# Seven half-size block products for eight in the gate/up stages of a float32 decoder trunk

## The chip, the core and the metric

The kernel runs on one core of one Trainium2 chip. Its time is the device time of one execution in microseconds (us); the number given for a kernel is the median of several runs. Five engines work side by side, each through its own list of instructions in a fixed order: PE (TensorE, matrix products), DVE (VectorE) and ACT (ScalarE) (element by element), POOL (GpSimd, element by element, SBUF only) and SP, which here issues the loads. They wait for one another by semaphores only.

## The reference

Two layers work on 512 tokens of width 1024 in float32. Each layer has four sub-layers: a SwiGLU feed-forward network with weight 1/2, a token mixer, a second such network, and a gated embedding. All of them are normalised before and after, and added to the residual. The change touches the feed-forward networks alone, of which there are four:

```python
def swiglu(x, w_gate, w_up, w_down):
    return (jax.nn.silu(x @ w_gate) * (x @ w_up)) @ w_down

h = rmsnorm(x, g_ffn1_pre[i])
x = x + 0.5 * rmsnorm(swiglu(h, w1_gate[i], w1_up[i], w1_down[i]), g_ffn1_post[i])
```

`w_gate` and `w_up` are 1024 x 2816, `w_down` is 2816 x 1024.

## The kernel before

**Layout.** Activations lie with features on the 128 partitions and tokens in the columns: 1024 features are eight slabs of 128 x 512 (`xs`), the 2816 hidden features 22 slabs (`hid`). A weight tile of 128 x 128 is the stationary operand of a matrix product, 512 tokens (or 256, where a stage is done in token halves) are the moving one.

**Exact halves.** Every float32 operand is cut in two: `h`, its rounding to a shorter type that PE takes at full rate, and `l`, what is left. A product of two operands is three matmuls into one PSUM bank: high by high, low by high, high by low (`product`, lines 255 to 257). ACT makes the high part (`halves`, line 239, `wh`), DVE or POOL the low part by a subtraction (line 240, `wl`); the letter `on` says which engine. For an activation `split` does the same (lines 174 and 175, `h` and `l`). Every weight is loaded once (`load_raw`, 256 KB a load, line 233, four buffers) and has its halves made in eight buffers of 128 x 512 for `wh` and eight for `wl`.

**A feed-forward network** (`ffn`) is a gate/up stage and a down stage. The gate/up stage goes over 22 M-tiles of 128 hidden features. Each has a gate product and an up product over all eight slabs of `xs`: 2 x 8 x 3 = 48 matmuls of 512 columns, with four loads of weights and their halves. `activate` then multiplies both PSUM banks by `rb`, the tokens' 1/rms as a row on every partition (lines 556 and 558, DVE), applies silu (line 557, ACT), multiplies gate by up (line 559, DVE), and cuts the result in halves. The down stage has eight M-tiles of 22 x 3 = 66 matmuls; the last is done in two token halves, so that the post-norm of the first half runs beside the products of the second (`finish`).

**Entry.** `Entry` brings the residual `x` up to date slab by slab, first for tokens 0 to 255, then for 256 to 511, and makes its halves (`xh` on ACT, line 415; `xl` on DVE, line 418). The first three products of the next stage follow slab by slab in token halves (`products`); a fourth needs no `rb`. The sums of squares give `rb` some time later.

**What sets the order.** The loads, the matmuls and the element-wise work are written in the order of the program; a list scheduler of the framework then fixes each engine's order when the kernel is built, within the limits of the buffers. Only a few stretches are pinned by hand (`manual_schedule`, `issue_after`).

Of the kernel before, what the change touches and what calls it, by code (L numbers as in the profile page):

```python
# [34 lines left out]
# M-tiles done in token halves where a sub-layer starts and where it ends  # L35
# [6 lines left out]
# engines of the first weights' differences  # L42
# [10 lines left out]
# engines (a, v, g) of the mixer's copies and differences  # L53
# [24 lines left out]
HID_TAGS = {"s": "m" * 8 + "a" * 10 + "s" * 4, "m": "a" * 10 + "s" * 12}  # L78
# [7 lines left out]
# output projection: order of the K-slabs, and how many of them each M-tile takes early  # L86
# [10 lines left out]
# columns of the small-parameter array, per layer  # L97
# [10 lines left out]
# columns of the constants array  # L108
# [26 lines left out]
def hybrid_trunk(ctx: ExitStack, tc: tile.TileContext, a: dict, out: bass.AP):  # L135
# [83 lines left out]
    # ---- weights: DMA, then exact halves  # L219
    def load_w(src, slabs, cols, on="vv"):  # L220
# [3 lines left out]
        return [w for k0 in range(0, slabs, per)  # L224
                for w in halves(load_raw(src[:, k0:min(k0 + per, slabs)], cols), on[k0 // per % len(on)])]
# [5 lines left out]
    def load_raw(src, cols):  # L231
        raw = wtile("raw", src.shape[1], cols, F32)
        nc.sync.dma_start(out=raw, in_=src)
        return raw

    def halves(raw, on="v"):
        _, n, cols = raw.shape
        h, lo = wtile("wh", n, cols, F32R), wtile("wl", n, cols, F32R)
        A.copy(out=h, in_=raw)  # L239
        (G if on == "g" else V).tensor_tensor(out=lo, in0=raw, in1=f(h), op=ALU.subtract)  # L240
        return [(h[:, k], lo[:, k]) for k in range(n)]
# [6 lines left out]
    def product(o, w, xs, first=True, cols=slice(0, S), tick=lambda: None, last=True):  # L248
        """o[:, cols] = sum over slabs; a bank's later columns are not `first`."""
# [10 lines left out]
    def start():  # L260
        """The first normalized input and the first weights, as they arrive."""
# [25 lines left out]
        first = [(w[t, 0] + w[t, 1], bank()) for t in range(3)]  # L287
# [7 lines left out]
        rt, rb = rstd(sq.parts(), D)  # L295
        return SimpleNamespace(xs=xs, rt=rt, rb=rb, first=first)

    # ---- norms
    def rsqrt_cols(o, v4, inv_d, between):
# [10 lines left out]
        mul, add, sub = ALU.mult, ALU.add, ALU.subtract  # L310
        for op, kw in (
            (V.tensor_scalar, dict(out=v, in0=v4, scalar1=inv_d * lam, scalar2=EPS * lam, op0=mul, op1=add)),
# [11 lines left out]
            between()  # L324

    class Rstd:
# [3 lines left out]
        def __init__(self, dim, cols=slice(0, S), tag="v"):  # L330
            self.dim, self.blocks, self.st, self.tag = dim, blocks(cols), None, tag

# [10 lines left out]
        def col(self, between=lambda: None):  # L343
            n = len(self.blocks)
            self.rt = tp.tile([P, n], F32, tag=f"rt{n}", name="rt", bufs=4)
            rsqrt_cols(self.rt, self.st, 1.0 / self.dim, between)
# [9 lines left out]
    def rstd(sqs, dim, tag="v"):  # L356
        r = Rstd(dim, tag=tag)
# [9 lines left out]
    class Squares:  # L367
        """Sums of squares over M-tiles, for the tokens `cols`."""
# [29 lines left out]
    class Entry:  # L398
        """A sub-layer's input: x * gain as exact halves, and rstd. `update(k, cols)` first brings
        x[k] up to date; `row_b()` makes what it needs for the later half of the tokens."""  # L400
# [25 lines left out]
        def products(self, tiles, more=lambda: None):  # L426
            """tiles: (weights, bank) of the first M-tiles, in token halves; `more()`: further
            products that need no rstd."""
# [11 lines left out]
            r = Rstd(D)  # L440
# [8 lines left out]
        def later(self):  # L449
            """Conversions of later weights queue behind those of the input."""  # L450
# [5 lines left out]
    def finish(ys, sq, last, compute, evac, gcol, nxt, at, xtag="s"):  # L456
        """The last M-tiles in token halves, each half's post-norm during the other's products;
        then the residual, and the next sub-layer's input."""
        rb = slot(name="rbs")
        direct = {m: slot(name="sq") for m in list(last)[-DIRECT:]}  # L460
# [13 lines left out]
        ra, rb_ = Rstd(D, ca), Rstd(D, cb)  # L474
# [28 lines left out]
        def row_b():  # L503
            rb_.row(rb[:, cb], None)
# [40 lines left out]
    # ---- sub-layers  # L545
    def ffn(l, idx, state, nxt, xtag="s", early=None):
        xs = state.xs
        hid, banks = [], {}
        order = [(m, j) for m in range(NF) for j in range(2)]

        def weights(m, j, on="vv"):
            return load_w(a[f"w{idx + 1}_gu"][l, m, j], NK, P, on)

        def activate(m):
            g1, u1 = slot(name="g1"), slot(name="u1")
            V.tensor_tensor(out=g1, in0=banks[m, 0], in1=rb, op=ALU.mult)  # L556
            A.activation(out=g1, in_=g1, func=AF.Silu)
            V.tensor_tensor(out=u1, in0=banks[m, 1], in1=rb, op=ALU.mult)  # L558
            V.tensor_tensor(out=u1, in0=g1, in1=u1, op=ALU.mult)  # L559
            hid.append(split(u1, HID_TAGS[xtag][m]))  # L560

        def one(m, j):
            w, b = weights(m, j), bank()
# [3 lines left out]
        def more():  # L567
            for t in order[FIRST:FIRST + MORE]:
                with state.later():
                    w = weights(*t)  # L570
                banks[t] = bank()
                product(banks[t], w, xs)

        done = len(order[:FIRST])
        if l == 0 and idx == 0:
            first = state.first
            round_constants()
        else:
            first = [(weights(*t, on), bank()) for t, on in zip(order[:FIRST], (ON_FFN1, ON_FFN2)[idx].split())]
            state.products(first, more)  # L580
            done += MORE
# [3 lines left out]
        for i, (m, j) in enumerate(order):  # L585
            if (m, j) == (2, 0) and early is not None:
                early()
            if i >= done:
                one(m, j)
            if j:  # L590
                activate(m)
# [6 lines left out]

        for m in range(NK - LAST_DOWN):
            o = bank()  # L600
            product(o, down(m), hid)
# [17 lines left out]
        return finish(ys, sq, last, compute, evac, lambda k: half[:, l, idx, k:k + 1], nxt, AT_DOWN)  # L619

    def trig():
        """cos and signed sin of the rotary angles, [32 * 4 rows, tokens]"""
# [48 lines left out]
    # stick-breaking attention, scores transposed: keys on partitions  # L671
    def sb_head(h, q, k, v, mix):
# [5 lines left out]
        # banks of key blocks; columns are queries j*P .. S  # L678
# [132 lines left out]
    def mixer(l, state, nxt):  # L811
# [51 lines left out]
        # stick-breaking values and the rotary key, tokens on partitions  # L863
# [304 lines left out]
```

## Time and profile before

| | |
|---|---|
| runs of the kernel before | 2185.63, 2184.93, 2184.9 us; median 2184.93 |
| profiled execution, first to last instruction | 2182.0 us (its own device time is not listed; the span is 2.9 us under the median) |
| PE / PEld | 2113.9 us (97%) / 1797.3 us (82%), 10672 matmuls |
| DVE, ACT, POOL | 1264.4 us (58%), 888.5 us (41%), 381.4 us (17%) |
| mean granted PE clock | 0.986 |
| read from memory | 183.65 MB, 85 GB/s over the span |

The page of a profile gives busy times by engine, a chart of 40 slices, and the chain of work that ended last. The groups list instructions of one line, engine and shape with their number, busy time, mean duration in ns and the idle time ahead of them. The timeline gives starts and durations; like rows that follow one another are merged, with their count. The windows give busy time by engine in a stretch. A matmul's recorded duration covers its way through the array, so that matmuls overlap in the records: what one costs is the distance from its start to the next one's.

### The profile page before, as it was taken

To read this page: it belongs to the slowest core of one execution; us is meant where nothing else is said; L and a number is where in the kernel's file an instruction comes from. 1 tells how busy PE (TensorE), PEld (TensorE's weight loads), DVE (VectorE), ACT (ScalarE), POOL (GpSimd) and SP (SyncE) were. 2 spreads that over 40 slices of the span, in tenths; PEclk is the share of its full clock that TensorE was granted. 3 is DMA by queue.
4 is the path that set the end of the run, shared out by engine and by line. 5 is a ranking of instruction groups with operands and counts; after the bars stand their busy time and mean duration, and the time that the engine had idled before them with its cause. 6 is when DMAs were issued, how large, how long until landed. Compare 5 with 4: busy or idle time off the path is not lost.

```text
span 2182.0 us, 29065 instructions
## 1 busy us (share of the span) xinstructions
PE 2113.9 (97%) x10672; PEld 1797.3 (82%) x10672; DVE 1264.4 (58%) x2291; ACT 888.5 (41%) x1696; POOL 381.4 (17%) x354
## 2 busy tenths in 40 slices
PE   8999999999999999999999999999999999999996
PEld 7888888887888888888888888888878888888886
DVE  7644434878877444336774443357788764443376
ACT  5333323545554333224543332235555543332243
POOL 1000002126331000003320000031263400000043
PEclk9999999999999999999899999999999999999998
DMA  5222332311113223332222233322111132223322
GB/s 181 97 97 97 93 98 71 95 55 50 54 42 104 97 97 97 92 100 80 78 93 97 98 97 92 97 67 97 56 53 47 44 107 97 96 95 96 96 73 68
DMA packets 108286, 187.63 MB, mean 86 GB/s; under 512 B 12144, under 2 KB 22640, under 8 KB 108144
## 3 DMA queue, kind: packets, MB, share of 16 engines
q1 hardware_dynamic: 107424, 185.12, 26.9%
q8 instruction: 83, 1.36, 0.2%
q10 hardware_dynamic: 720, 0.67, 0.1%
q14 instruction: 59, 0.48, 0.1%
HBM read 183.65 MB, written 2.10 MB: 85 GB/s over the span
## 4 chain that ended last, share of the span: by engine, by line
PE 86%; DVE 11%; ACT 1%; issue 1%; DMA 0%; POOL 0%; DVEq 0%; ACTq 0%; POOLq 0%
PE ps L256 22%; PE ps L257 22%; PE ps L255 22%; DVE x L516 2%; PE in L255 2%; PE in L256 2%; PE in L257 2%; DVE xl L418 2%; DVE wl L240 1%; PE wo L255 1%; PE wo L256 1%; PE wo L257 1%; PE st L340 1%; DVE y L513 1%; PE z L718 1%
## 5 line engine op out<-in xcount | busy, mean ns | idle before, releaser
L239 ACT CAST wh<-raw 128x512 fp32r<-128x512 f32 (+3 forms) x718 | 428.3, 602 | 818.6 <-PE ps L256 710.8
L240 DVE TENSOR_TENSOR wl<-raw,wh 128x512 fp32r<-128x512 f32 (+3 forms) x677 | 468.5, 697 | 479.8 <-ACT wh L239 476.8
L256 PE MATMUL ps<-xl,wh 128*128 128x512 f32 (+1 forms) x1688 | 627.5, 374 | 11.6 <-DVE xl L418 11.6
L255 PE MATMUL ps<-xh,wh 128*128 128x512 f32 (+1 forms) x1688 | 618.0, 374 | 9.6 <-ACT wh L239 6.6
L257 PE MATMUL ps<-xh,wl 128*128 128x512 f32 (+1 forms) x1688 | 625.5, 372 | 0.0
L392 POOL TENSOR_TENSOR sq<-sq 128x256 f32<-128x256 f32 (+1 forms) x165 | 170.7, 1036 | 1573.3 <-ACT sq L382 1570.5
L256 PEld LDWEIGHTS ps<-xl,wh 128*128 128x128 f32 x1688 | 321.6, 191 | 68.7 <-DVE xl L418 14.8
L255 PEld LDWEIGHTS ps<-xh,wh 128*128 128x128 f32 x1688 | 318.4, 191 | 65.1 <-ACT wh L239 6.6
L257 PEld LDWEIGHTS ps<-xh,wl 128*128 128x128 f32 x1688 | 321.7, 191 | 54.2 <-DVE wl L240 0.3
L255 PE MATMUL ps<-h,wh 128*128 128x512 f32 (+1 forms) x824 | 302.6, 367 | 0.0
L256 PE MATMUL ps<-l,wh 128*128 128x512 f32 (+1 forms) x824 | 302.2, 367 | 0.4 <-DVE l L175 0.4
L257 PE MATMUL ps<-h,wl 128*128 128x512 f32 (+1 forms) x824 | 302.0, 367 | 0.0
L256 PEld LDWEIGHTS ps<-l,wh 128*128 128x128 f32 x824 | 155.4, 189 | 26.1 <-DVE l L175 1.1
L257 PEld LDWEIGHTS ps<-h,wl 128*128 128x128 f32 x824 | 155.4, 189 | 25.4 <-DVE wl L240 0.5
L255 PEld LDWEIGHTS ps<-h,wh 128*128 128x128 f32 x824 | 155.4, 189 | 25.1
L558 DVE TENSOR_TENSOR u<-ps,rb 128x512 f32<-128x512 f32 x88 | 60.7, 690 | 115.4 <-PE ps L257 115.4
L556 DVE TENSOR_TENSOR g<-ps,rb 128x512 f32<-128x512 f32 x88 | 60.8, 690 | 113.9 <-PE ps L257 111.9
L256 PE MATMUL in<-xl,wh 128*128 128x512 f32 (+1 forms) x288 | 103.1, 363 | 4.6 <-DVE xl L418 4.6
L257 PE MATMUL in<-xh,wl 128*128 128x512 f32 (+1 forms) x288 | 102.5, 361 | 0.0
L255 PE MATMUL in<-xh,wh 128*128 128x512 f32 (+1 forms) x288 | 99.8, 366 | 1.5 <-ACT xh L415 1.5
L174 ACT CAST h<-u 128x512 fp32r<-128x512 f32 x88 | 54.5, 620 | 112.6 <-DVE u L559 112.5
L175 DVE TENSOR_TENSOR l<-u,h 128x512 fp32r<-128x512 f32 x88 | 60.5, 691 | 50.9 <-ACT h L174 50.9
(284 smaller groups left out, 2589.4 us busy)
## 6 DMA issues: line engine op xcount, KB each, us to landing
raw<-in_w_gu SPq DMA_DIRECT2D x352, 256.0 KB, 2.5
raw<-in_w_down SPq DMA_DIRECT2D x160, 256.0 KB, 2.6
raw<-in_win_f SPq DMA_DIRECT2D x60, 256.0 KB, 2.7
raw<-in_ple_gate SPq DMA_DIRECT2D x32, 256.0 KB, 2.6
raw<-in_wo_a SPq DMA_DIRECT2D x18, 256.0 KB, 2.8
raw<-in_w_down SPq DMA_DIRECT2D x32, 128.0 KB, 2.1
raw<-in_wo_b SPq DMA_DIRECT2D x12, 256.0 KB, 2.7
raw<-in_win_t SPq DMA_DIRECT2D x16, 144.0 KB, 2.2
```

The costliest lines, as they stand in the source:

```text
L174: A.copy(out=h, in_=src)
L175: V.tensor_tensor(out=lo, in0=src, in1=f(h), op=ALU.subtract)
L239: A.copy(out=h, in_=raw)
L240: (G if on == "g" else V).tensor_tensor(out=lo, in0=raw, in1=f(h), op=ALU.subtract)
L255: T.matmul(oc, wh, xh[:, cols], start=first and k == 0, stop=False, **kw)
L256: T.matmul(oc, wh, xl[:, cols], start=False, stop=False, **kw)
L257: product.last = T.matmul(oc, wl, xh[:, cols], start=False, stop=last and k == n - 1, **kw)
L392: G.tensor_tensor(out=self.acc[:, c], in0=self.acc[:, c], in1=self.last[:, c], op=ALU.add)
L418: iv = V.scalar_tensor_tensor(out=lo, in0=x[k][:, c], scalar=g, in1=f(h), op0=ALU.mult, op1=ALU.subtract)
L516: V.scalar_tensor_tensor(out=x[k][:, c], in0=ys[k][:, c], scalar=gcol(k), in1=x[k][:, c], op0=ALU.mult, op1=ALU.add)
L556: V.tensor_tensor(out=g1, in0=banks[m, 0], in1=rb, op=ALU.mult)
L558: V.tensor_tensor(out=u1, in0=banks[m, 1], in1=rb, op=ALU.mult)
```

## The change

Take one M-tile. Let the input be cut in four blocks, a11, a12, a21, a22: the first index is the token half (256 tokens each), the second the half of the 1024 features (four slabs each). Let the weights be cut in b11 (gate, first four slabs), b21 (gate, last four), b12 and b22 (the same for up). Gate is a11 b11 + a12 b21 and a21 b11 + a22 b21 for the two token halves, up the same with b12 and b22: eight block products. The changed kernel uses the seven-product form of Strassen and Winograd for M-tiles 2 to 21 (class `Unit`, 20 of 22 in each of four stages):

- input forms, once a stage (`input_forms`): s1 = a21 + a22, s2 = a11 - s1, s3 = a11 - a21, s4 = a12 + s2, each with its exact halves (`fh`, `fl`);
- weight forms, for every unit: t1 = b12 - b11, t2 = t1 - b22, t3 = b22 - b12, t4 = b21 + t2. Seven operands (b11, b21, b22, t1 to t4) then need their exact halves, where four did;
- seven products p1 to p7 of 4 slabs x 3 matmuls of 256 columns. p1, p6, p5 and p3 run on in one PSUM bank (`ux`), p7 and p4 in another (`uy`), p2 in a third (`uz`); after each of p1, p6, p5 and p3 ACT copies the running sum out, after p2, p5 and p4 DVE adds.

`ON_FORM` puts the low parts of b11, b21, b22 and t3, and the subtraction that makes t3, on POOL, the rest on DVE. In the first two units of a stage all of it is on DVE (`ON_FORM_NEW`). `up` is no longer multiplied by `rb`: the missing factor by token goes through down into the post-norm, whose epsilon is divided by the same factor (`eps`, a few operations on 128 x 4 values).

The hidden values of the units are kept whole, in one slot each, and cut in halves only ahead of down (`late`). Down's first two M-tiles run side by side, hidden slab by hidden slab (`TOGETHER`). M-tiles 0 and 1 stay plain.

```diff
+    class Unit:
...
+        def __init__(self, src, forms, z, tag, form_on, t3_on):
+            self.forms, self.tag, self.form_on, self.t3_on = forms, tag, form_on, t3_on
+            self.raw = {n: load_raw(src[j][:, k0:k0 + 4], P, tag)
+                        for n, j, k0, tag in (("b11", 0, 0, None), ("b21", 0, 4, None),
+                                              ("b12", 1, 0, "a"), ("b22", 1, 4, "a"))}
...
+        def form(self, n):
+
+            r = self.raw
+            if n == "t2":
+                r["t1"], r["t2"] = (aslot(name="tw").rearrange("p (a b) -> p a b", a=4) for _ in range(2))
+                tt("v", r["t1"], r["b12"], r["b11"], ALU.subtract)
+                tt("v", r["t2"], r["t1"], r["b22"], ALU.subtract)
+            elif n == "t3":
+                r["t3"] = r["b12"]
+                tt(self.t3_on, r["t3"], r["b22"], r["b12"], ALU.subtract)
+            elif n == "t4":
+                r["t4"] = r["b21"]
+                tt("v", r["t4"], r["b21"], r["t2"], ALU.add)
+            return halves(r[n], self.form_on[n])
...
+            for k, ((wh, wl), (xh, xl)) in enumerate(zip(w, self.forms[xn])):
+                T.matmul(o, wh, xh, start=first and k == 0, stop=False, **kw)
+                T.matmul(o, wh, xl, start=False, stop=False, **kw)
+                T.matmul(o, wl, xh, start=False, stop=k == 3, **kw)
...
+        def p4(self, rb):
+            o, g = self.product("y", "t4", "a22", False), self.g
+            V.tensor_tensor(out=g[:, 256:512], in0=o, in1=g[:, 256:512], op=ALU.add)
+            V.tensor_tensor(out=g, in0=g, in1=rb, op=ALU.mult)
+            A.activation(out=g, in_=g, func=AF.Silu)
+            V.tensor_tensor(out=g, in0=g, in1=self.u, op=ALU.mult)
+            return g
...
-            V.tensor_tensor(out=u1, in0=banks[m, 1], in1=rb, op=ALU.mult)
-            V.tensor_tensor(out=u1, in0=g1, in1=u1, op=ALU.mult)
-            hid.append(split(u1, HID_TAGS[xtag][m]))
+            V.tensor_tensor(out=g1, in0=banks[m, 1], in1=g1, op=ALU.mult)
+            hidden(g1)
...
+            if u:
+                u.p1()
+                u.p2()
+            if prev:
+                prev.p3()
+            if u:
+                u.p6()
+            if prev:
+                hidden(prev.p4(rb))
+            if u:
+                u.p7()
+                u.p5()
+            prev = u
+        hid += [split(h, t) for h, t in zip(late, HID_HALVES[EARLY_HID:])]
...
+        together = [bank() for _ in range(TOGETHER)]
```

How the engines' orders move is seen at three places. The first is DVE in the middle of a gate/up stage (first network of layer 0). Before, one M-tile has eight instructions there: four low parts of weights, the two products with `rb`, gate by up, and the low part of the result.

```order
L240 TENSOR_TENSOR wl<-raw,wh 128x512 x2
L558 TENSOR_TENSOR u_1222<-ps,rb 128x512
L240 TENSOR_TENSOR wl<-raw,wh 128x512
L559 TENSOR_TENSOR u_1222<-g_1221,u_1222 128x512
L175 TENSOR_TENSOR l<-u_1222,h 128x512
L240 TENSOR_TENSOR wl<-raw,wh 128x512
L556 TENSOR_TENSOR g_1305<-ps,rb 128x512
```

Now a unit has eleven there. `tw` is t1 or t2, `raw<-raw,tw` is t4, `wl` a low part; `uy` and `uz` are PSUM banks; `g1` and `u1` are the gate and up values of a unit, and the numbers tell buffers apart.

```order
L182 TENSOR_TENSOR tw_2454<-raw_2395,raw_2391 128x512
L263 TENSOR_TENSOR wl_2318<-tw_2314,wh_2317 128x512
L182 TENSOR_TENSOR raw_2252<-raw_2252,tw_2314 128x512
L263 TENSOR_TENSOR wl_2336<-raw_2111,wh_2335 128x512
L182 TENSOR_TENSOR tw_2455<-tw_2454,raw_2397 128x512
L688 TENSOR_TENSOR g1_1976<-uy_2078,g1_1976 128x256
L689 TENSOR_TENSOR g1_1976<-g1_1976,rb_273 128x512
L263 TENSOR_TENSOR wl_2374<-tw_2313,wh_2373 128x512
L691 TENSOR_TENSOR g1_1976<-g1_1976,u1_1977 128x512
L182 TENSOR_TENSOR tw_2595<-raw_2536,raw_2532 128x512
L681 TENSOR_TENSOR u1_2118<-uy_2219,u1_2118 128x256
L670 TENSOR_TENSOR g1_2258<-uz_2282,g1_2258 128x256
```

Eight of the eleven read two operands from SBUF, all 128x512 (t1, t2, t4, three low parts, the product with `rb`, gate by up; the tenth row shown is already the next unit's t1); the other three read a PSUM bank and one operand from SBUF, 128x256.

The second place is POOL in the same stretch. Before, it has nothing there. Now each unit has five instructions on it: the low parts of b11, b21, b22 and t3, and the subtraction that makes t3 (`raw<-raw,raw`).

```order
L263 TENSOR_TENSOR wl_2402<-raw_2391,wh_2401 128x512
L263 TENSOR_TENSOR wl_2420<-raw_2393,wh_2419 128x512
L182 TENSOR_TENSOR raw_2536<-raw_2538,raw_2536 128x512
L263 TENSOR_TENSOR wl_2438<-raw_2256,wh_2437 128x512
L263 TENSOR_TENSOR wl_2498<-raw_2395,wh_2497 128x512
```

All five are 128x512 and read both operands from SBUF.

The third place is DVE at the entry to the second network of layer 0, between the last slab of the input (`xl_7370`, slab 7 in the later token half) and the low part of the first unit's t2 (`wl_7864`), which its third product p6 waits for. `xg` and `s2` are the input's forms in the making, `fl` their low parts.

```order
L453 SCALAR_TENSOR_TENSOR xl_7370<-x7_80,gains_71,xh_7369 128x256
L182 TENSOR_TENSOR xg_7734<-xg_7734,s2_7743 128x512
L182 TENSOR_TENSOR fl_7747<-s2_7743,fh_7746 128x512
...
L182 TENSOR_TENSOR xg_7767<-xg_7767,s2_7776 128x512
...
L182 TENSOR_TENSOR tw_7859<-raw_7817,raw_7813 128x512
...
L670 TENSOR_TENSOR g1_7821<-uz_7845,g1_7821 128x256
L182 TENSOR_TENSOR tw_7860<-tw_7859,raw_7819 128x512
L182 TENSOR_TENSOR raw_7817<-raw_7819,raw_7817 128x512
...
L263 TENSOR_TENSOR wl_7864<-tw_7860,wh_7863 128x512
```

These are nine of the rows; in full there are 14 instructions with two SBUF operands of 128x512 after `xl_7370` up to `wl_7864`, one from PSUM, and five of the short ones (128x4) that make `rb`. Before, low parts of plain weights stood there, and no product waited for the whole input.

More of the change, by code (lines that the diff above doesn't have):

```diff
@@ L286, in start @@
             part(k + 1)
-        first = [(w[t, 0] + w[t, 1], bank()) for t in range(3)]
+        first = [(w[t, 0] + w[t, 1], bank("ps", PLAIN_BANKS[t])) for t in range(3)]
         for k in range(NK):
@@ L294, in start, with rsqrt_cols @@
         sq.fold()
-        rt, rb = rstd(sq.parts(), D)
-        return SimpleNamespace(xs=xs, rt=rt, rb=rb, first=first)
-    def rsqrt_cols(o, v4, inv_d, between):
+        eps = eps_col()
+        rt, rb = rstd(sq.parts(), D, keep=eps)
+        return SimpleNamespace(xs=xs, rt=rt, rb=rb, first=first, eps=eps)
+    def rsqrt_cols(o, v4, inv_d, between, eps=None, keep=None):
         c0, c1 = 0.703952253, 2.38924456
@@ L324, in rsqrt_cols, with __init__ @@
             between()
+        if keep is not None:
+            V.tensor_scalar(out=keep, in0=v, scalar1=EPS, scalar2=None, op0=mul)
     class Rstd:
-        def __init__(self, dim, cols=slice(0, S), tag="v"):
+        def __init__(self, dim, cols=slice(0, S), tag="v", eps=None, keep=None):
             self.dim, self.blocks, self.st, self.tag = dim, blocks(cols), None, tag
+            self.kw = dict(eps=eps if eps is None else eps[:, cols.start // P:cols.stop // P], keep=keep)
         def add(self, *sqs, last=False, cols=None):
@@ L543, in finish, with input_forms, scaled_x, keep @@
         return Entry(*nxt, update, row_b, xtag)
+    def input_forms(l, name, xs, xtag):
+        tag = "m" if xtag == "s" else "s"
+        made = {n: [] for n in ("s1", "s2", "s3", "s4")}
+        c1, c2 = HALVES
+        def scaled_x(k, c):
+            t = aslot(name="xg").rearrange("p (a b) -> p a b", a=2)
+            for i in range(2):
+                A.activation(out=t[:, i], in_=x[k + i][:, c], func=AF.Copy, scale=gain(l, name, k + i))
+            return t.rearrange("p a b -> p (a b)")
+        def keep(n, t, on):
+            h, lo = slot(F32R, "fh", tag), slot(F32R, "fl", tag)
+            A.copy(out=h, in_=t)
+            tt(on, lo, t, f(h), ALU.subtract)
+            made[n].append((h, lo))
+        for k in (0, 2):
+            a11, a12 = scaled_x(k, c1), scaled_x(k + 4, c1)
+            a21, a22 = scaled_x(k, c2), scaled_x(k + 4, c2)
+            s1, s2 = a22, aslot(name="s2")
+            tt("g", s1, a21, a22, ALU.add)
+            tt("v", s2, a11, s1, ALU.subtract)
+            keep("s2", s2, "v")
+            tt("g", a21, a11, a21, ALU.subtract)
+            keep("s3", a21, "v")
+            keep("s1", s1, "g")
+            tt("v", a12, a12, s2, ALU.add)
+            keep("s4", a12, "v")
+        def pieces(n):
+            if n[0] == "s":
+                return [(h[:, i * 256:i * 256 + 256], lo[:, i * 256:i * 256 + 256])
+                        for h, lo in made[n] for i in range(2)]
+            c = HALVES[int(n[1]) - 1]
+            k0 = 4 * (int(n[2]) - 1)
+            return [(h[:, c], lo[:, c]) for h, lo in xs[k0:k0 + 4]]
+        return {n: pieces(n) for n in ("a11", "a12", "a22", "s1", "s2", "s3", "s4")}
@@ L546, in ffn, with hidden @@
     def ffn(l, idx, state, nxt, xtag="s", early=None):
         xs = state.xs
-        hid, banks = [], {}
-        order = [(m, j) for m in range(NF) for j in range(2)]
+        hid, late, banks = [], [], {}
+        order = [(m, j) for m in range(PLAIN) for j in range(2)]
+        src = a[f"w{idx + 1}_gu"]
         def weights(m, j, on="vv"):
-            return load_w(a[f"w{idx + 1}_gu"][l, m, j], NK, P, on)
+            return load_w(src[l, m, j], NK, P, on)
+        def hidden(h):
+            if len(hid) < EARLY_HID:
+                hid.append(split(h, HID_HALVES[len(hid)]))
+            else:
+                late.append(h)
@@ L584, in ffn @@
             banks[t] = b
[L585 to L591, printed above, removed]
+        for t in order[done:]:
+            one(*t)
+        forms = input_forms(l, f"ffn{idx + 1}_pre", xs, xtag)
+        for m in range(PLAIN):
+            activate(m)
+        if early is not None:
+            early()
+        prev = None
+        for m in range(PLAIN, NF + 1):
+            new = m < PLAIN + NEW_UNITS
+            u = None
+            if m < NF:
+                u = Unit(src[l, m], forms, "df"[m % 2], HID_WHOLE[m], ON_FORM_NEW if new else ON_FORM,
+                         ON_T3_NEW if new else ON_T3)
+            if u:
[12 more added lines that the diff above has]
+        hid += [split(h, t) for h, t in zip(late, HID_HALVES[EARLY_HID:])]
+        turn[0] += 2 * NF + (l + idx > 0)
         sq, ys = Squares(), {}
```

116 lines of the change are left out of this document (88 added, 28 removed).

## Prediction

> **What bounds the kernel now.** I read the page first: its busy times and the chain that ended last.
>
> ```profile
> span 2182.0 us, 29065 instructions
> PE 2113.9 (97%) x10672; PEld 1797.3 (82%) x10672; DVE 1264.4 (58%) x2291; ACT 888.5 (41%) x1696; POOL 381.4 (17%) x354
> PE 86%; DVE 11%; ACT 1%; issue 1%; DMA 0%; POOL 0%; DVEq 0%; ACTq 0%; POOLq 0%
> ```
>
> PE is the bound, and the chain lies on it for 86% of the span. These are averages, so next come the windows of two gate/up stages (first and second network of layer 0).
>
> ```profile
> core 0: us, PE busy (x) PEld busy (x) DVE busy (x) ACT busy (x) POOL busy (x), PEclk, DMA share, GB/s
> 49.00:245.00 196.00, 196.00 (x866) 162.31 (x865) 104.03 (x165) 69.58 (x113) 0.00 (x0) 1.00 0.30 96
> 700.00:895.00 195.00, 195.00 (x862) 161.47 (x861) 93.06 (x145) 66.19 (x108) 0.00 (x0) 1.00 0.29 95
> ```
>
> There PE has no gap at full clock, DVE works half of the time, ACT a third, POOL not at all. 862 matmuls of 512 columns in 195 us are 0.226 us each; what PE no longer has to do there shortens the kernel until another engine is late. What a matmul of 256 columns costs stands in the timeline of a down stage, which ends in token halves: first and last row of a gapless run of each width.
>
> ```profile
> 334.61 0.39 PE L257 MATMUL ps<-h,wl 128*128 128x512 f32 x1
> 353.65 0.39 PE L257 MATMUL ps<-h,wl 128*128 128x512 f32 x1
> 353.88 0.28 PE L255 MATMUL ps<-h,wh 128*128 128x256 f32 x1
> 361.19 0.28 PE L256 MATMUL ps<-l,wh 128*128 128x256 f32 x1
> ```
>
> 84 steps lie between the first two starts: 0.2267 us each. 61 steps lie between the last two: 0.120 us. Half the columns cost 53%, with new weights for every matmul.
>
> **PE's part.** Before, 48 wide matmuls an M-tile: 48 x 0.2267 = 10.88 us. After, 7 x 4 x 3 = 84 narrow ones: 84 x 0.120 = 10.08 us. That is 0.80 us less for each of 80 units: **-64.1 us**. One eighth less arithmetic would have been 1.36 us a unit; the narrow matmul's surcharge takes the rest.
>
> **ACT, memory, PSUM, down.** These are the groups by shape that the other engines' work is priced with.
>
> ```profile
> L239 ACT CAST wh<-raw 128x512 fp32r<-128x512 f32 x654 | 402.7, 621 | 734.9 <-PE ps L256 643.7 <-DVE wl L240 18.4 <-PE in L256 14.9
> L240 DVE TENSOR_TENSOR wl<-raw,wh 128x512 fp32r<-128x512 f32 x615 | 433.9, 711 | 419.4 <-ACT wh L239 418.1 <-issue 0.3
> L557 ACT ACTIVATE g<-g 128x512 f32<-128x512 f32 x88 | 55.6, 632 | 23.4 <-DVE g L556 23.4
> L239 ACT CAST wh<-raw 128x256 fp32r<-128x256 f32 x36 | 14.7, 409 | 67.5 <-PE ps L256 67.1 <-PE wo L256 0.4
> L240 POOL TENSOR_TENSOR wl<-raw,wh 128x512 fp32r<-128x512 f32 x39 | 52.3, 1345 | 78.3 <-ACT wh L239 78.1
> L1048 DVE TENSOR_TENSOR part<-wo,part 128x256 f32<-128x256 f32 x32 | 12.4, 418 | 6.3 <-PE wo L257 6.1
> ```
>
> ACT per unit: seven casts at 0.62, four copies of 256 columns at about 0.41 (nearest row: a cast of that size), silu 0.63, the hidden value's cast 0.62: 7.2 us of 10.08. Hidden behind PE, nothing; three more casts a unit would end that. Loads keep their number and size: 96 GB/s at a DMA share of 0.30 become about 104, nothing. The running sum in `ux` makes p6 wait for the copy after p1; p2's 1.44 us cover the copy's 0.4, and so on around the unit: nothing. Down: 20 hidden values cut late cost ACT 12.4 and DVE 14.2 us, beside eleven weight loads' halves (6.8 and 7.8), while two M-tiles give PE 132 x 0.2267 = 29.9 us. Both fit: nothing, at most 2 us a stage where the last unit's values come late. The product of up with `rb` leaves DVE, which was not the bound.
>
> **DVE and POOL in the stage.** Taken one by one they fit. DVE has eight instructions at 0.71 and three at 0.42, 6.9 us of 10.08; POOL five at 1.345, 6.7 us. But all five of POOL's and eight of DVE's read two operands from SBUF, and the trace has a place where both engines have such work waiting (layer 0's start; two engines' timelines, a row of x2 merges two instructions).
>
> ```profile
> 24.38 3.48 DVE L240 TENSOR_TENSOR wl<-raw,wh 128x512 fp32r<-128x512 f32 x2
> 26.08 2.38 DVE L240 TENSOR_TENSOR wl<-raw,wh 128x512 fp32r<-128x512 f32 x2
> 27.78 1.28 DVE L240 TENSOR_TENSOR wl<-raw,wh 128x512 fp32r<-128x512 f32 x2
> 17.84 1.29 POOL L392 TENSOR_TENSOR sq<-sq 128x512 f32<-128x512 f32 x1
> 20.59 3.31 POOL L392 TENSOR_TENSOR sq<-sq 128x512 f32<-128x512 f32 x2
> 23.98 3.32 POOL L392 TENSOR_TENSOR sq<-sq 128x512 f32<-128x512 f32 x2
> ```
>
> DVE's starts are 1.70 us apart (24.38, 26.08, 27.78), and so are POOL's (20.59 to 23.98 is two steps). One pair takes 1.70 us, as if the two took turns. After POOL's last one DVE goes on at 0.60 us a step (1.28 for two, less the 0.68 that one takes alone); POOL alone takes 1.29. So they do not overlap. A unit with five POOL turns needs five pairs and three more DVE steps: 5 x 1.70 + 3 x 0.60 = **10.30 us**, if the three instructions with a PSUM operand run inside POOL's turns. That is more than PE's 10.08 and less than the old 10.88. Below 10.08 it cannot go. Without any packing it is 8 x 0.60 + 5 x 1.345 = 11.5. I take 10.35, near the lower end, since the eight `wl` buffers let both engines run a whole unit ahead of PE and so keep work waiting on each: +0.27 for the 72 units that use POOL, **+19 us** (0 to +102).
>
> Here a rule of the Trainium skill speaks against the change: SBUF — State Buffer, section Who interferes with whom, says that a VectorE instruction with two SBUF inputs and a GpSimd instruction that reads SBUF exclude one another for the whole instruction. With recorded durations it would give 8 x 0.711 + 5 x 1.345 = 12.4 us a unit, 167 us more than PE's time. The trace agrees on the turns, and not on that sum: a pair takes 1.70, less than 0.71 + 1.345 = 2.06.
>
> **Entry into a stage.** Before, products need the input slab by slab. Now p6 needs s2, which needs all of it. The timeline at the second network's entry, layer 0, and two of the short steps:
>
> ```profile
> 667.59 0.95 DVE L418 SCALAR_TENSOR_TENSOR xl<-x,gains,xh 128x256 fp32r<-128x256 f32 x1
> 32.58 0.15 DVE L323 TENSOR_SCALAR r_v<-st 128x4 f32<-128x4 f32 x1
> 32.77 0.17 DVE L323 TENSOR_SCALAR r_y<-r_v 128x4 int32<-128x4 int32 x1
> ```
>
> and, from the windows, the same entry as a whole (PE idle for 2.74 of 60 us, clock 0.94):
>
> ```profile
> 640.00:700.00 60.00, 57.26 (x316) 50.68 (x317) 46.94 (x93) 31.43 (x63) 18.05 (x21) 0.94 0.27 87
> ```
>
> At 668.5 the last slab is there. By the new order DVE then has 14 two-operand steps (8.4 us), one PSUM step (0.3 to 0.42) and five short ones (about 0.2 apart) up to t2's low part: 9.7 us, and POOL makes the other forms in the meantime, four turns of 1.1 us (1.70 less 0.60) that can be in the way: 9.7 to 14.1. PE has the rest of the plain products (six narrow, two wide), four sums of squares, p1 and p2: some 4.2 us. It stands for 5.5 to 9.9 us; I take one turn in the way, 6.6. For the second unit's p6 DVE has 11 + 4 steps of 0.60 and five short ones, 10.0 us, beside five products of PE, 7.2: 2.8 us more. Together 9.4 us (5.5 to 14; the top holds a stretch at lower clock after the gap, of which the window above shows the kind) at each of three entries: **+28 us**. At the first stage the input is there early; the forms add DVE 16 steps and POOL six in a stretch that is already crowded (rows above): **+4 us** (0 to 8).
>
> **Sum.** -64.1 + 19.4 + 28 + 4 = -12.7 us on the profiled 2182.0; its own device time is not known, so I put the same on the median, 2184.93: **2172 us**.
>
> **Rivals.** (1) DVE and POOL pack badly. Each waits for casts on ACT, whose list holds copies that wait for PE, and a turn lost is not made up. Against the likely case speaks that 10.30 asks for a pair of engines that never idle. At 11.5 us a unit it is 72 x 1.42 = 102 us on top: -64 + 102 + 32 = +70, 2255 us. It decides from (64.1 - 32) / 72 = 0.45 over PE's time: from 10.53 us a unit on the change loses. This is the Trainium skill's rule at work, short of its full sum. Chance 0.33, 2190 to 2255.
> (2) PE stays the bound in the stage, because turns fall where DVE would wait anyway: -64.1 + 32 = -32 us, 2153; with the cheapest entries (3 x 5.5, 0 at the first) 2137. For it: DVE idles half of the old stage. Against: 10.30 is over 10.08 before any loss. Chance 0.15, and the forecast, 2155 to 2180, has 0.40.
> (3) The gains and losses meet, 10.47 to 10.6 us a unit, within 0.2% of 2184.93 (4.4 us, about what a measurement of this kernel can tell from no change). Chance 0.12.
> That the change does not do what it says is no case here: the orders show 6720 narrow matmuls in place of 3840 wide ones.
>
> **Numbers.** Faster by over 0.2%: 0.40 + 0.15 = 0.55; same 0.12; slower 0.33. The range goes from 2135 (PE-bound stages, cheap entries) to 2235, which is 11.2 us a unit with entries as taken; a tenth at either side is left out. The likely case's own range is 2155 to 2180.
>
> **What would show it.** In the changed profile, units u4 to u17 of a stage should follow one another at about 10.35 us with PE gaps released by DVE or POOL `wl`. POOL's mean on the new low parts should be above 1.345 us or DVE's two-operand rows above 0.71, whichever waits; were both as alone, the turns are wrong. At the three later entries PE should stand for 6 to 10 us ahead of the first p6, released by DVE. No gaps in either place mean 2150 or less; units of 10.6 us or more mean a loss. Gaps ahead of down, or PE waiting for ACT's copies, would be something that I put at nothing.

## The result, and the profile after

The changed kernel takes **2314.61 us** (median of 4 runs, 2312.71 to 2317.52) beside 2184.91 us for the kernel before in the same session: a ratio of 1.0594, 95% interval 1.0579 to 1.0609. It is 130 us slower, on the other side of what was forecast and 80 us above the top of the range.

The page first: span, busy times, and the engines' shares of the chain that ended last.

```profile
span 2315.7 us, 36714 instructions
PE 2115.4 (91%) x13552; PEld 1913.3 (83%) x13552; DVE 1733.6 (75%) x2691; ACT 1125.1 (49%) x2352; POOL 981.8 (42%) x738
PE 56%; DVE 27%; issue 5%; ACT 5%; DMA 1%; POOL 1%; DVEq 0%; ACTq 0%; SPq 0%; POOLq 0%
```

PE's share of the chain went from 86% to 56%, DVE's from 11% to 27%. Next the windows: the first 69 us of the stage in layer 0's first network, then the second network of layer 0, which had no PE gap before, at its start, in steady work, in its middle and towards its end.

```profile
core 0: us, PE busy (x) PEld busy (x) DVE busy (x) ACT busy (x) POOL busy (x), PEclk, DMA share, GB/s
31.00:100.00 69.00, 47.51 (x329) 44.92 (x328) 59.61 (x93) 25.76 (x52) 29.63 (x18) 0.88 0.20 65
713.00:760.00 47.00, 35.37 (x257) 33.38 (x256) 40.53 (x61) 23.68 (x47) 18.77 (x11) 0.89 0.18 62
770.00:850.00 80.00, 77.82 (x617) 74.95 (x617) 68.56 (x81) 40.37 (x87) 53.51 (x37) 1.00 0.28 93
856.00:890.00 34.00, 27.84 (x218) 27.44 (x218) 33.12 (x31) 14.88 (x31) 26.58 (x17) 0.90 0.29 97
890.00:953.00 63.00, 53.02 (x425) 51.20 (x424) 51.49 (x60) 32.56 (x69) 36.40 (x24) 1.00 0.22 69
```

80 us at 0.120 us a matmul would hold 667; 617 are there, so PE loses 6 us in the steady part although its idle time shows only 2.2: records of 0.28 us overlap at a step of 0.12, and a gap below the difference doesn't show. The other windows lose more, and after the gaps the granted clock is below 1.

From PE's timeline, the distance from each unit's first matmul to the one 84 unit matmuls later, in us (second network of layer 0; the first value holds plain matmuls and the rest of the entry too):

```
26.5 11.8 10.6 10.8 10.6 11.0 11.0 11.0 11.0 11.0 11.0 11.3 17.9 10.1 11.6 12.2 12.7 12.0 14.1
```

From the fifth unit on the other stages look the same; in the first stage units 2 and 4 take 18.5 and 15.6 as well. PE's time is 10.08. Where the rest goes shows in the groups by shape of the engines that read two operands from SBUF.

```profile
L263 POOL TENSOR_TENSOR wl<-raw,wh 128x512 fp32r<-128x512 f32 x327 | 506.6, 1569 | 305.9 <-ACT wh L262 273.9 <-PE uz L661 14.8 <-DVE wl L263 11.2
L263 DVE TENSOR_TENSOR wl<-tw,wh 128x512 fp32r<-128x512 f32 x160 | 172.6, 1079 | 13.9 <-ACT wh L262 13.9
L182 DVE TENSOR_TENSOR tw<-tw,raw 128x512 f32<-128x512 f32 x80 | 114.4, 1430 | 0.6
L689 DVE TENSOR_TENSOR g<-g,rb 128x512 f32<-128x512 f32 x80 | 99.9, 1249 | 2.1
```

POOL's low parts take 1.569 us in place of 1.345, and DVE's two-operand steps 1.08 to 1.43 in place of 0.71. That is what it looks like if each waits for the other inside its instructions; the experiments below test it. One steady unit on DVE's timeline, then two rows of ACT and PE and two of POOL:

```profile
800.27 0.42 DVE L688 TENSOR_TENSOR g<-uy,g 128x256 f32<-128x256 f32 x1 [0.68 <-PE uy L661]
800.73 1.82 DVE L689 TENSOR_TENSOR g<-g,rb 128x512 f32<-128x512 f32 x1
803.24 1.01 DVE L691 TENSOR_TENSOR g<-g,u 128x512 f32<-128x512 f32 x1 [0.70 <-ACT g L690]
804.17 0.68 DVE L182 TENSOR_TENSOR tw<-raw 128x512 f32<-128x512 f32 x1
804.77 0.41 DVE L681 TENSOR_TENSOR u<-uy,u 128x256 f32<-128x256 f32 x1
805.11 1.67 DVE L182 TENSOR_TENSOR tw<-tw,raw 128x512 f32<-128x512 f32 x1
806.70 0.41 DVE L670 TENSOR_TENSOR g<-uz,g 128x256 f32<-128x256 f32 x1
...
809.08 1.54 DVE L263 TENSOR_TENSOR wl<-tw,wh 128x512 fp32r<-128x512 f32 x1 [0.17 <-ACT wh L262]
811.30 0.42 DVE L688 TENSOR_TENSOR g<-uy,g 128x256 f32<-128x256 f32 x1 [0.68 <-PE uy L661]
```

```profile
806.86 0.62 ACT L262 CAST wh<-tw 128x512 fp32r<-128x512 f32 x1 [1.90 <-DVE tw L182]
807.54 0.39 PE L659 MATMUL ux<-fh,wh 128*128 128x256 f32 x1 [0.35 <-ACT wh L262]
799.00 4.69 POOL L263 TENSOR_TENSOR wl<-raw,wh 128x512 fp32r<-128x512 f32 x3
804.93 1.30 POOL L182 TENSOR_TENSOR raw<-raw 128x512 f32<-128x512 f32 x1 [1.23 <-DVE tw L182]
```

This is a closed round of 11.03 us (800.27 to 811.30). In it the chain that ended last goes through DVE's list from p4's sum to t2 (800.27 to 806.8, with silu on ACT in between), through ACT's cast of t2 (806.86) and through PE's products of p6 and p4 (807.54 to 811.3) back to p4's sum. DVE stands still three times, for 0.68 (p4's product on PE), 0.70 (silu) and 0.17 us: 1.55 us in which POOL works and DVE can pair nothing. Four of its steps meet a POOL step and take 1.0 to 1.8 us, three of them on that chain (800.73, 803.24, 805.11). Against 0.60 us each they cost it 2.5 us; without these it would be 8.5 us long, an estimate from these rows, and PE's 10.08 would decide. And in DVE's list are the steps that empty PSUM (`g<-uy,g`, `u<-uy,u`, `g<-uz,g`), without which PE can't start its next product. In the middle of the stage this becomes a long stop (DVE, POOL, PE):

```profile
858.69 1.79 DVE L182 TENSOR_TENSOR tw<-raw 128x512 f32<-128x512 f32 x1
860.40 1.78 DVE L263 TENSOR_TENSOR wl<-tw,wh 128x512 fp32r<-128x512 f32 x1
...
867.17 1.74 DVE L691 TENSOR_TENSOR g<-g,u 128x512 f32<-128x512 f32 x1
868.84 1.74 DVE L182 TENSOR_TENSOR tw<-tw,raw 128x512 f32<-128x512 f32 x1
870.50 0.41 DVE L681 TENSOR_TENSOR u<-uy,u 128x256 f32<-128x256 f32 x1
```

```profile
856.47 6.86 POOL L263 TENSOR_TENSOR wl<-raw,wh 128x512 fp32r<-128x512 f32 x4
863.30 1.74 POOL L182 TENSOR_TENSOR raw<-raw 128x512 f32<-128x512 f32 x1
864.99 5.04 POOL L263 TENSOR_TENSOR wl<-raw,wh 128x512 fp32r<-128x512 f32 x3
```

```profile
864.55 0.28 PE L661 MATMUL ux<-fh,wl 128*128 128x256 f32 x1
870.97 0.58 PE L659 MATMUL uy<-xh,wh 128*128 128x256 f32 x1 [6.14 <-DVE u L681]
```

POOL does eight steps in a row; DVE goes at one step in 1.66 to 1.71 us beside it, seven times, and only then comes to `u<-uy,u`, for which PE has waited 6.14 us. Each of the four stages has one such stop, of 6.14 to 6.16 us.

### The profile page after: what moved, and what is told of

Same layout as the page of the kernel before. It is cut to its first block, busy times and chain, and to the rows that moved or that the text cites. A ratio compares the mean times of both kernels' runs of the same rounds, so it can differ in the third digit from the quotient of the medians.

```text
span 2315.7 us, 36714 instructions
## 1 busy us (share of the span) xinstructions
PE 2115.4 (91%) x13552; PEld 1913.3 (83%) x13552; DVE 1733.6 (75%) x2691; ACT 1125.1 (49%) x2352; POOL 981.8 (42%) x738
## 4 chain that ended last, share of the span: by engine, by line
PE 56%; DVE 27%; issue 5%; ACT 5%; DMA 1%; POOL 1%; DVEq 0%; ACTq 0%; SPq 0%; POOLq 0%
PE ps L279 8%; PE ps L278 8%; PE ps L280 8%; DVE wl L263 5%; DVE tw L182 5%; PE ux L659 3%; PE ux L661 3%; DVE x L553 3%; DVE g L689 3%; PE ux L660 2%; PE uy L659 2%; DVE xl L453 2%; PE in L279 2%; PE in L278 2%; PE in L280 2%
## 5 line engine op out<-in xcount | busy, mean ns | idle before, releaser
L262 ACT CAST wh<-raw 128x512 fp32r<-128x512 f32 (+2 forms) x798 | 465.9, 601 | 400.2 <-PE ps L279 271.3
L263 POOL TENSOR_TENSOR wl<-raw,wh 128x512 fp32r<-128x512 f32 x329 | 508.3, 1565 | 311.7 <-ACT wh L262 279.7
L263 DVE TENSOR_TENSOR wl<-raw,wh 128x512 fp32r<-128x512 f32 (+2 forms) x469 | 347.3, 749 | 291.1 <-ACT wh L262 263.3
L659 PE MATMUL ux<-fh,wh 128*128 128x256 f32 x960 | 280.9, 293 | 48.7 <-ACT wh L262 34.8
L661 PE MATMUL ux<-fh,wl 128*128 128x256 f32 x960 | 278.6, 290 | 5.2 <-DVE wl L263 5.2
L660 PE MATMUL ux<-fl,wh 128*128 128x256 f32 x960 | 275.2, 287 | 1.1 <-DVE fl L182 1.0
L659 PEld LDWEIGHTS ux<-fh,wh 128*128 128x128 f32 x960 | 187.4, 195 | 59.7 <-ACT wh L262 41.5
L661 PEld LDWEIGHTS ux<-fh,wl 128*128 128x128 f32 x960 | 187.3, 195 | 7.9 <-DVE wl L263 7.6
L660 PEld LDWEIGHTS ux<-fl,wh 128*128 128x128 f32 x960 | 187.6, 195 | 2.1 <-DVE fl L182 1.6
L263 DVE TENSOR_TENSOR wl<-tw,wh 128x512 fp32r<-128x512 f32 x160 | 172.6, 1079 | 13.9 <-ACT wh L262 13.9
```

The source lines that it names most:

```text
L659: T.matmul(o, wh, xh, start=first and k == 0, stop=False, **kw)
L660: T.matmul(o, wh, xl, start=False, stop=False, **kw)
L661: T.matmul(o, wl, xh, start=False, stop=k == 3, **kw)
```

## The experiments

The theory ahead of them: POOL's and DVE's turns at SBUF cost most of the loss. Its rivals: the operands' forms are simply too much work for DVE and ACT, wherever they run; or the starts of the stages cost it. Times are medians; the kernel before ran beside them at 2183.5 to 2183.8 us.

**All forms on DVE.** POOL's five steps of a unit go to DVE, which then has 16 in a unit.

```diff
-ON_FORM = {"b11": "g", "b21": "g", "b22": "g", "t1": "v", "t2": "v", "t3": "g", "t4": "v"}
-ON_T3 = "g"
+ON_FORM = {"b11": "v", "b21": "v", "b22": "v", "t1": "v", "t2": "v", "t3": "v", "t4": "v"}
+ON_T3 = "v"
```

> All eighteen later units like the first two: the low parts and the t3 subtraction that were on POOL are on DVE, 13 two-operand steps of 0.60 us and three short ones a unit, 8.8 us of PE's 10.08; POOL has nothing in the stage. Nothing is left out. Theory A (DVE and POOL take turns at SBUF, and DVE's list, which also empties PSUM, stands behind POOL): units at 10.1 to 10.6 us, the 6 us gap in mid-stage gone, 2185 to 2215 us. Theory B (DVE simply has too much to do, or the way cast - low part - product is too long, whoever makes the low parts): units at 11 us or more, 2310 us or above, since DVE gets 3 us more a unit. Theory C (narrow matmuls are dearer than 0.120 us in this stage): 2300 us, hardly moved.

Measured 2210.52 us, ratio 1.0113 (1.0093 to 1.0133): 104 us come back by giving the loaded engine more instructions, as the theory expected (2185 to 2215). Its window of steady work, and the groups that answer to those above:

```profile
770.00:850.00 80.00, 80.00 (x665) 79.82 (x664) 75.05 (x133) 46.37 (x97) 0.00 (x0) 1.00 0.35 119
```

```profile
L263 DVE TENSOR_TENSOR wl<-tw,wh 128x512 fp32r<-128x512 f32 x160 | 109.4, 684 | 1.0
L182 DVE TENSOR_TENSOR tw<-tw,raw 128x512 f32<-128x512 f32 x80 | 54.9, 687 | 1.3
L689 DVE TENSOR_TENSOR g<-g,rb 128x512 f32<-128x512 f32 x80 | 54.9, 687 | 1.2
```

The same steps are back at 0.69 us, PE holds 665 matmuls where 667 fit, the units take 10.08 to 10.17 from the fifth on, and the stop in the middle is gone. DVE is busy for 94% of that window: it is close to being the bound by itself.

**POOL's steps taken away.** Their low parts become copies on ACT, and t3 is b12; DVE's work stays as in the changed kernel.

```diff
-        (G if on == "g" else V).tensor_tensor(out=lo, in0=raw, in1=f(h), op=ALU.subtract)
+        if on == "c":
+            A.copy(out=lo, in_=raw)
+        else:
+            (G if on == "g" else V).tensor_tensor(out=lo, in0=raw, in1=f(h), op=ALU.subtract)
```

> POOL's five instructions a unit are taken out of its hands and DVE gets none of them: the low parts of b11, b21, b22 and t3 are copies made by ACT in place of differences, and t3 is b12, so the numbers of the result change; DVE's own eleven instructions stay. Theory A: DVE's two-operand rows return to 0.69 us, units at 10.1 to 10.4 us, 2170 to 2200 us (ACT has 9.3 us a unit now, which may cost some). Theory B: DVE's work and order are the same, so units stay at 11 us, 2280 us or more. Theory C: the same as B.

Measured 2207.93 us (1.0106, 1.0086 to 1.0127), as with all on DVE, and 8 us above what was expected. From the seventh unit on most take 10.1 to 10.4, so what is left lies mostly at the stages' starts, where the first unit takes 24 to 28 us. What POOL's help costs is the help itself: doing this work on DVE costs no more than hardly doing it at all. ACT, busy for 1269 us in it, is not the bound.

**POOL reading SBUF for nobody.** All forms on DVE, and POOL subtracts raw weights from themselves into a tile that nothing reads, five times a unit. The tile takes one of 35 slots away.

```diff
+            for j in {"b11": ("b11",), "b21": ("b21",), "t3": ("b22", "b22"), "b22": ("b22",)}.get(n, ()):
+                q = r[j].rearrange("p a b -> p (a b)")
+                tt("g", junk, q, q, ALU.subtract)
```

> All low parts on DVE, nothing left out; besides, POOL subtracts a loaded weight tile from itself into a tile that nobody reads, five times in each of the 20 units (b11, b21, b22 three times); one slot of 35 gives the room. POOL's work is in nobody's chain. Theory A (turns at SBUF): DVE's two-operand rows go from 0.69 to over 1 us, a unit needs up to 5 x 1.70 + 8 x 0.60 = 13.3 us, 2380 to 2470 us. Theory D (the loss came from waiting for POOL's slow low parts, not from DVE being held up): 2205 to 2220 us, as without.

Measured 2538.95 us (1.1626, 1.1603 to 1.1649), 328 us more than with POOL idle and above even the range expected of the turns. A steady unit takes 14.08 us; DVE's timeline has it from one `g<-uy,g` to the next, 876.02 to 890.10, with POOL's five below.

```profile
882.26 2.13 DVE L264 TENSOR_TENSOR wl<-raw,wh 128x512 fp32r<-128x512 f32 x2
884.31 1.52 DVE L264 TENSOR_TENSOR wl<-tw,wh 128x512 fp32r<-128x512 f32 x1
885.76 4.42 DVE L264 TENSOR_TENSOR wl<-raw,wh 128x512 fp32r<-128x512 f32 x3
890.10 0.41 DVE L692 TENSOR_TENSOR g<-uy,g 128x256 f32<-128x256 f32 x1
```

```profile
882.75 6.88 POOL L182 TENSOR_TENSOR junk<-raw 128x512 f32<-128x512 f32 x5 [7.20 <-DMA raw<-in_w_gu]
```

While POOL runs, DVE's steps start 1.45 us apart (884.31, 885.76) in place of 0.60. Five times 0.85 is 4.25 us, and the unit is 3.92 us longer than 10.16. No product waits for POOL here, and DVE stands for 0.69 us of the round (silu), no more than without POOL's reads; what grew is the time of its own steps. So it is the turns that cost the time. The first two runs alone left another explanation, that taking steps off POOL changes the order of everything else; here DVE has the same steps as in the 2210.52 us kernel.

**One, three or five steps on POOL.** The low part of b22 alone, or those of b11, b21 and b22, on POOL; the rest on DVE. Two theories of the turns are told apart: S, that only the sum of SBUF time in a unit counts, and O, that DVE's steps which empty PSUM must not stand behind runs of turns.

```diff
-ON_FORM = {"b11": "v", "b21": "v", "b22": "v", "t1": "v", "t2": "v", "t3": "v", "t4": "v"}
+ON_FORM = {"b11": "g", "b21": "g", "b22": "g", "t1": "v", "t2": "v", "t3": "v", "t4": "v"}
```

> The same with one instruction a unit on POOL, the low part of b22. Sum 8.3 us a unit. Theory S: 2205 to 2220 us, units of 10.1 to 10.2 us. Theory O: a single turn delays one DVE step by 1.1 us and no run of turns can form, so also 2205 to 2225 us; above 2230 neither holds. If POOL's help were a gain at this dose (DVE relieved of one step in 13), 2200 or less.

> A dose between the changed kernel (five instructions a unit on POOL, 2314.6 us) and the one with all on DVE (2210.5 us): the low parts of b11, b21 and b22 on POOL, t3 and its low part on DVE. By the turns a unit needs n x 1.70 + (13 - 2n) x 0.60 us of SBUF time for n POOL instructions: 7.8 with none, 9.3 with three, 10.3 with five. If only the sum counts (theory S), three fit under PE's 10.08: units of 10.1 to 10.3 us, no gap in the middle of a stage, 2205 to 2225 us. If what hurts is that DVE's steps which empty PSUM stand behind runs of turns (theory O), a gap in the middle stays and the time lies between the two, 2240 to 2290 us.

Measured 2207.69 us with one (1.0114, 1.0098 to 1.0129) and 2258.47 with three (1.0352, 1.0334 to 1.037), against 2210.52 with none and 2314.61 with five. One step is worth nothing either way. Three cost 48 us, where theory S expected none: their sum is 9.3 us a unit, and the steady units take 10.65, with one unit of 13 to 14.5 us in the middle of each stage. So the sum of SBUF time does not decide, and theory O's range held. Its mechanism is there only in part, as PE's waits in the second stage with three steps on POOL show (780 to 920 us):

```profile
PE uy L661 <- DVE wl L263: 1.8, 1, 1.8
PE uy L659 <- DVE g L688: 1.6, 2, 0.9
```

Late low parts cost as much there as late emptying of PSUM (`g<-uy,g`). In the steady units two of the turns fall on the chain told above: `g<-g,rb` takes 1.33 and `g<-g,u` 1.01 us (at 795.21 and 797.25). That these two make the 10.65 was not tried apart.

**Only the products.** No forms of input or weights; each unit's seven products use the four raw blocks and their halves, on DVE.

```diff
-        for k in (0, 2):
+        for k in ():
...
+            n = {"t1": "b12", "t2": "b11", "t3": "b12", "t4": "b21"}.get(n, n)
+            if n not in self.made:
+                self.made[n] = halves(self.raw[n], "v")
+            return self.made[n]
```

> Input forms and weight forms are left out: the seven products use the halves of b11, b21, b12 and b22, four a unit, all on DVE as before the change; the result is another. What is left is PE's part of the change. Theories A and B: 84 matmuls at 0.120 us, units at 10.08 us, 2185 - 64 = 2121 us, 2112 to 2135. Theory C: units well over 10.08 us without any of the added work, 2185 us or more.

Measured 2125.05 us (0.9727, 0.9706 to 0.9748): 58 us under the kernel before, units of 10.08. 58 of PE's 64 us are there. Two windows at stage starts of this kernel, and the like ones of the kernel with all forms on DVE:

```profile
31.00:100.00 69.00, 67.95 (x564) 67.53 (x563) 49.51 (x93) 34.48 (x71) 0.00 (x0) 1.00 0.34 110
656.00:703.00 47.00, 46.41 (x386) 46.12 (x386) 27.70 (x55) 23.15 (x47) 0.00 (x0) 1.00 0.33 113
```

```profile
31.00:100.00 69.00, 51.49 (x321) 49.19 (x320) 59.30 (x104) 25.60 (x52) 8.95 (x6) 0.78 0.20 65
690.00:737.00 47.00, 35.84 (x252) 34.44 (x251) 39.49 (x70) 23.80 (x47) 6.68 (x4) 0.85 0.18 62
```

With the forms, 243 and 134 matmuls fewer fit in: at 0.120 us, 29 us in the first stage and 16 us at a later entry. The granted clock falls to 0.78 and 0.85 there.

**Input forms left out**, once in the changed kernel and once with all on DVE (s1 to s4 are the raw blocks).

```diff
-        for k in (0, 2):
+        for k in ():
...
-        return {n: pieces(n) for n in ("a11", "a12", "a22", "s1", "s2", "s3", "s4")}
+        made_of = {"s1": "a21", "s2": "a11", "s3": "a12", "s4": "a22"}
+        return {n: pieces(made_of.get(n, n)) for n in ("a11", "a12", "a22", "s1", "s2", "s3", "s4")}
```

> The input forms s1 to s4 are left out; blocks of the input stand in their place, so the result is another, and p6 no longer waits for the whole input. The units are as in the change. All theories: the gaps at the entries (6.5 us ahead of the first p6) go, 10 to 14 us a stage, 2260 to 2275 us; the mid-stage gap and 11 us units stay under A. If much more goes, the entry is the main cause; if nothing goes, the entry was hidden.

> All low parts on DVE, and the input forms left out as well (blocks of the input in their place, so the result is another): the entry's price without POOL's turns in the units. With the forms the first unit alone took 27 to 29 us of which 10.1 are its own. If the entry is the second cause, some 12 to 15 us go at each of three entries and up to 30 at the first, 60 to 75 us off 2210: 2135 to 2150 us. If the rest is DVE's load in the units, 2195 us or more.

Measured 2305.99 us with POOL in use (1.0555, 1.051 to 1.0601) and 2171.41 with all on DVE (0.9943, 0.9923 to 0.9963). The first is a miss: the gap ahead of the first p6 went (first unit of the later stages 13.6 us in place of 25 to 27), yet many of the units that follow rose to 12 to 14 us in three of the four stages, and 9 us were left of the gain. On DVE alone the same edit brings 39 us, a gain, but less than the 60 to 75 expected. Why the units grew was not settled; since one stage with the same work has units of 11.03, it is not the amount of work. The other 46 us between 2171.4 and 2125.05 are the weights' forms; 17 of the 76 timed units then take 10.83.

**More plain M-tiles at the start**, all forms on DVE: three, then four in place of two, with PSUM banks to match; with four, the first three are activated ahead of the fourth's products.

```diff
-PLAIN = 2
+PLAIN = 4
...
-PLAIN_BANKS = "zsfz"
+PLAIN_BANKS = "fszzdsfs"
```

> All low parts on DVE, and three plain M-tiles ahead of the units in place of two, so that PE has 10.9 us more to do while the input forms are made; 19 units a stage. Nothing is left out. If the gap at the entry is DVE's list (10 forms and their low parts) in front of p6, a plain tile with seven DVE steps buys PE 10.9 us for 4.2 of DVE: some 6 to 7 us a stage less, 0.8 a stage given back, 2180 to 2192 us. If the entry is only moved, 2205 to 2215.

> All low parts on DVE, four plain M-tiles ahead of 18 units, the fourth once the first banks are free. As with three, twice: 12 us a stage less than with two, 2160 to 2180 us, faster than the kernel before by up to 1%. If the entry is only moved, 2205 to 2220.

Measured 2181.53 us with three (0.9993, 0.9983 to 1.0003), the same as the kernel before, and 2173.62 with four (0.9946, 0.993 to 0.9961), half a per cent faster than it. Each plain M-tile gives up 0.8 us of PE's gain, and the cover that it gives the forms is worth more. Then the same four plain M-tiles with POOL in use as in the changed kernel; and, with all forms on DVE again, six of them in the first stage:

```diff
+        plain = 6 if l == 0 and idx == 0 else PLAIN
```

> The engines of the changed kernel (five a unit on POOL) with four plain M-tiles a stage in place of two, as in the variant with all on DVE that took 2173.6 us. If the entry and the turns are separate costs, the turns take 16 units of 18 in place of 18 of 20, 104 x 16/18 = 92 us over 2173.6: 2255 to 2280 us. If the turns cost only because the stage begins late and out of step, the longer plain start heals them too: under 2220 us.

> The variant with all on DVE and four plain M-tiles a stage (2173.6 us), with six plain ones in the first stage alone, whose first three units there took 30.5, 12.9 and 14.9 us beside 10.88 us of plain products, about 17 us over PE's time. If that is the input's forms meeting the first weights on DVE, two more plain M-tiles (1.6 us) win 8 to 15 us of it: 2160 to 2168 us. If it is something that the plain M-tiles do not cover, 2173 to 2177 us.

Measured 2277.19 us (1.0439, 1.0417 to 1.046) and **2159.36 us** (0.9892, 0.9877 to 0.9906), the fastest of all and just under the range expected. POOL's help costs 104 us with four plain M-tiles as with two: turns and entries are separate costs. The last one's first 69 us of the stage:

```profile
31.00:100.00 69.00, 67.89 (x384) 58.78 (x383) 60.48 (x102) 29.71 (x56) 9.61 (x6) 1.00 0.31 102
```

PE is busy for 67.89 us at full clock, where it was 47.51 in the changed kernel.

## Why the prediction was wrong

Measured, the 130 us are made up of the products (2183.5 to 2125.05: -58), the forms made by DVE (to 2210.5: +85), and POOL's part in them (to 2314.6: +104). The prediction had -64, +32 and +19.

**PE's part.** Right: -64.1 forecast, 58 of it measured with the products alone, and 84 matmuls take 10.08 us wherever nothing else is late.

**DVE and POOL in the stage.** The step that failed: "I take 10.35, near the lower end, since the eight `wl` buffers let both engines run a whole unit ahead of PE and so keep work waiting on each". The steady units take 11.03, and units 3 to 19 together 11.8 on the mean. The price of a pair, 1.70 us, held (1.66 to 1.71 from 858.69 to 870.50). What failed is that DVE could be kept packed. In the round shown (800.27 to 811.30) four of its steps beside POOL take 5.9 us, four alone 2.5, the three that read PSUM 1.1, and for 1.55 it stands: 11.0. The sum of 10.30 let the PSUM steps run inside POOL's turns, which only one of the three does in full, and had no term for standing. DVE's list goes in order and holds, between the low parts that may run ahead, steps that may not: p4's sum, the product with `rb`, silu's answer, gate by up. And the same list empties PSUM, so that a run of turns stops PE itself. The dose shows that fitting by sum is no proof: three steps on POOL sum to 9.3 and take 10.65.

Rival 1 was the one that came true, "DVE and POOL pack badly", beyond the point from which it decides (10.53). The reason that the prediction gave it is half of what the rows show: POOL waits for ACT's casts (2.38 us of a round by its timeline), but DVE does so for only 0.17 us; it stands for PE and for silu. Its price of 11.5 us a unit was near the measured 11.8, which holds the stops in mid-stage; with 32 us for the entries it gave 2255, and most of the missing 60 us are entries (44, below); the units' 11.8 in place of 11.5 is some 20. It had a chance of 0.33 because I weighed a lower bound against an unpacked sum and took the value near the bound. "Asks for a pair of engines that never idle" was the argument against my own case, and it held.

The Trainium skill, SBUF — State Buffer, section Who interferes with whom, has the two instructions exclude each other. The runs bear that out: useless POOL reads alone cost 328 us. Its full sum of 12.4 us a unit is above the steady 11.03, and a pair takes 1.70 and not 2.06. That its 167 us with the other terms as forecast come to 2320, close to 2315, is partly chance: the turns cost 104 against all forms on DVE, the entries 44 more than thought.

**Entry into a stage.** The stall ahead of the first p6 was forecast at 6.6 us; PE's timeline has 6.4 at two of the three later entries, ended by ACT's high part of t2, which waits for DVE's t2:

```profile
718.02 0.28 PE L661 MATMUL uz<-xh,wl 128*128 128x256 f32 x1
724.67 0.58 PE L659 MATMUL ux<-fh,wh 128*128 128x256 f32 x1 [6.37 <-ACT wh L262]
```

At the third, in layer 1's first network, PE waits 4.1 us for `rt`, from which `rb` is made, and 2.2 for the input's forms. The next term, 2.8 us for the second unit's p6, does not show: no recorded wait of PE between 740 and 770 is above 0.4 us. What the sum has no term for is that PE then waits for the products with `rb` that empty the plain M-tiles' banks, as its waits over the whole run show:

```profile
PE ux L659 <- ACT wh L262: 34.8, 33, 8.0
PE uy L659 <- DVE u L681: 25.8, 7, 6.2
PE uy L659 <- DVE g L688: 21.7, 19, 1.9
PE uz L659 <- DVE g L714: 6.8, 4, 2.2
PE ux L659 <- DVE g L714: 4.2, 3, 1.4
```

The last two rows are those banks, 11 us. With the lower clock after the gaps an entry costs some 16 us rather than 9.4 (713 to 760: 257 matmuls, against 386 in the like 47 us with the products alone). The first stage costs 28 (329 matmuls in place of 564) rather than 4: the forms there met a stretch where the low parts of the first weights already kept DVE busy, which the prediction had said ("already crowded") and priced too low. The six plain M-tiles there, worth 14 us, fit this. Together 28 + 3 x 16 = 76 us, 44 more than forecast; the ranges, 5.5 to 14 and 0 to 8, held neither.

**ACT, memory, down.** ACT's copies may be put at nothing as long as DVE keeps time: with all forms on DVE, and with POOL's steps taken away and ACT loaded more, no wait of PE for them shows. In the changed kernel PE waits for two of them, `u` (line 680) and `g` (line 673), 6.9 and 5.8 us over the run, a consequence that the prediction left out. Down itself was not tried apart.

**What would show it.** The signs named were the right ones: units of 10.6 us or more, POOL's low parts above 1.345, DVE's above 0.71.

Open: why the units grew when only the input's forms were left out, why the changed kernel's units take over 12 us towards a stage's end, and why the run of eight POOL steps forms where it does. The all-DVE kernel has neither; whether fewer free buffers for raw weights or the scheduler's order brings them was not tried.

## What to carry to other kernels

Ahead of giving a second engine part of the work, take the first's steps in their written order and ask which of them someone else waits for: where the two share SBUF, a step given away can cost the first engine more than doing it. A bound from summed times holds only for engines with nothing to wait for inside a round, so the silu's answer and the sum of the last product belong in the sum. Work that is made once at a stage's start has to be covered by products that don't need it: two to four plain M-tiles more turned the loss of the all-DVE version into a gain of 1.1%.

## What the runs showed of the hardware

- A 128x512 float32 step with two SBUF operands takes DVE 0.60 us from start to start alone and 1.70 beside a POOL step of that kind (1.66 to 1.71 in seven steps of the changed kernel); 1.45 where the POOL step reads one operand twice and nobody needs its result.
- In the changed kernel a POOL step saved DVE 0.60 us and still cost the kernel 104 / 360 = 0.29 us net; the useless ones cost 328 / 400 = 0.82 each.
- With PE gaps of 5.6 to 8 us, and shorter ones beside them, the granted clock in the 47 to 69 us around was 0.78 to 0.89, and 1.00 in the like stretches of the kernel with the products alone, where PE was busy for 98 to 99% of the time.
